# Output products of a hybrid encoder layer: which operand is halved where, one bank for the running sums, and a new order at both ends

## Chip, cores and metric

The kernel runs on one core of a Trainium2 chip. The metric is the device time of one execution in microseconds (us). Five engines work side by side, each through its own program in order: TensorE (PE in the profile; its weight loads, PEld, overlap the matmuls), VectorE (DVE), ScalarE (ACT), GpSimd (POOL) and SyncE (SP), which here issues the DMA transfers. They meet only in semaphores.

## What is computed

One encoder layer over x of 4096 rows by 1024:

```python
h = rmsnorm(x, pre_norm_g)
proj = h @ w_in                      # splits into q, k, v, g_a, u_p, g_p
a = banded_attention(q, k, v, rel_bias, sink) * silu(g_a)
p = multiscale_pool(u_p, pool_w, pool_scale) * silu(g_p)
mixed = concat([a, p]) @ w_out       # 1024 x 1024
x = x + rmsnorm(mixed, post_norm_g)
```

The attention is banded: each block of 128 queries sees its own block of keys and the two beside it, with a bias by distance and a sink term in the denominator. The pooling takes centred means over 2, 4, 8 and 16 rows, less the row itself.

## The kernel before

Every float32 operand of a matmul is split into a high and a low float16 part, and each product is high by high, high by low and low by high, summed in PSUM.

**First stage** (lines 135 to 796). It goes over x in eight macro-tiles of 512 rows. A tile of 128 rows is loaded (`x_load`), its mean square taken (`x_square`, `x_scale`), scaled and split (`x_high` on ScalarE, `x_low` on VectorE) and transposed by DMA (`x_turn`, line 193). Weight tiles are loaded (`w_load`), scaled by their column norm (`w_square`, `w_norm` on TensorE, `w_scale`, `w_scaled`) and split (`w_high`, `w_low`). Then 12 groups of 24 matmuls of 512 columns (`mm`, line 589) give the two gates and the pooling input; for the first macro-tile and first weight tile the matmuls run per 128 rows (`mm_first`, line 576), so that they can start on the first transposed tile. Gates and pooled blocks go to memory (`ga_scr`, `yp_scr`), and the output weights are brought into seven combinations for the second stage (`wo_scale`, `wo_sum1`, `wo_sum2`, `wo_keep`; into `w_scr`).

**Second stage** (from line 799). It goes over 32 blocks of 128 rows from the last to the first, in 16 pairs `u`. For each pair: projections of k, v and q (`do_kv`, `do_q`, line 831 and 965), two visits per block (`scores`, line 867, and a softmax in steps: `logits` on VectorE, line 888; `exps`, 899; `denominators`, 906; `probs` on ScalarE, 921; `rests` on VectorE, 929; `turn`, a DMA transpose issued by SP, 938), then `values` (1009) and `gate` (1017).

The output product of a pair is a 2 by 2 block product: its two row blocks by the two halves of K (attention and pooling), times the 2 by 2 blocks of `w_out`. It is done in seven products instead of eight, with sums of the operands: `sum1` to `sum4` build `s1` to `s4`, `pair` makes their high and low parts (`high` on ScalarE, `low` on GpSimd, line 1031), and `product` (line 1091) runs 12 matmuls of 512 columns. Before, the quarter named 11 is the attention of the odd block, 21 that of the even block, 12 and 22 are the pooled blocks. The blocks come in descending order, so the even block of a pair is ready last; products `11`, `22` and `12` do not need it, `s1` to `s4` do. The results are combined by `add` on VectorE (line 1123), squared, multiplied by the gain and added to x (`square`, `gain`, `mean`, `residual`, `store`).

**Order.** The order on all engines is written by hand: each step is put into `plan` by `due(t, step)`, and the steps are emitted in order of t. `pe(us, step)` puts a TensorE step at the running planned time `now[0]` and advances it; `visit` also keeps scores apart by `free`. The planned times set nothing but the order: on the chip each engine runs its program in order and waits for its operands. Three PSUM banks (`acc0` to `acc2`) are shared by projections and products.

Of the kernel before, what the change touches and what calls it, by code (L numbers as in the profile page):

```python
# [66 lines left out]
def hybrid_layer(ctx: ExitStack, tc, io, out):  # L67
# [67 lines left out]
    with ExitStack() as actx:  # L135
# [297 lines left out]
        def wo_load(kk):  # L433
            wo_t[kk] = pa.tile([P, D], F32, name=f"wo_b{kk}", tag="wraw", bufs=W_BUFS)
            nc.sync.dma_start(wo_t[kk], io["w_out"][kk])

        def wo_scale(kk):
            nc.scalar.activation(wo_t[kk], wo_t[kk], AF.Copy, scale=rowsc[:, kk : kk + 1])
# [203 lines left out]
        due(5.4, x_square, 0)  # L642
        due(6.6, w_square, 0)
        due(6.7, x_scale, 0)
        due(7.0, w_fold, 0, nc.gpsimd)
        due(7.6, x_high, 0)
        due(7.8, w_norm, 0, KT, gg)
        due(8.4, w_scale, 0)
        due(8.7, x_square, 1)
        due(8.8, x_low, 0)  # L650
        due(9.0, x_turn, 0)
        due(9.9, x_square, 2)
        due(10.0, x_scale, 1)
        due(10.4, w_scaled, 0)
        due(10.6, x_square, 3, nc.vector)
        due(10.7, w_high, 0)
        due(11.1, x_scale, 2)
        due(11.7, x_high, 1)
        due(11.8, w_low, 0)
        due(11.9, w_gate, 0)  # L660
        due(12.0, w_fold, 1, nc.gpsimd)
        due(12.8, x_low, 1)
        due(12.9, x_turn, 1)
        due(12.9, x_high, 2)
        due(13.0, x_scale, 3)
        due(14.2, x_low, 2)
        due(14.3, x_turn, 2)
        due(14.4, x_high, 3)
# [5 lines left out]
        due(14.35, lambda: nc.sync.dma_start(pw, io["pool_w"].rearrange("j p c -> p j c")))  # L674
        for j in range(2):
            due(15.9 + 0.1 * j, u_load, j)
        for i in range(BPM):
            due(14.0 + 1.3 * i + 1.5 * (i > 0), mm_first, i)
        due(15.5, w_norm, 1, KT)
        due(17.6, w_scale, 1)  # L680
        w_steps(1, 22.4)
        fold(2, 15.6)
        due(17.7, w_norm, 2, KT)
        due(18.8, w_scale, 2)
        w_steps(2, 25.0)
        fold(3, 18.8)
# [11 lines left out]
        def prepare(n):  # L698

            si = first[n + 2 :]  # L700
            if si:
                norm(si[0], 2 if A_GA <= si[0] < A_U else KT)
# [17 lines left out]
        now[0] = 21.0  # L720
        after(0, 0, 21.0)
# [258 lines left out]
    def proj_q(u, half):  # L980

        kv_t[u, half] = gemm.tile([P, 2, UT], F32, name=f"aq{u}_{half}", tag=f"acc{half}")
        for jj in range(2):
            project_t(kv_t[u, half][:, jj], B_Q + 2 * half + jj, x_half(u))
# [38 lines left out]
    def high(u, name, f):  # L1023

        tag = {"12": "s1", "22": "s3"}.get(name, name)
        y_t[u, name] = pb.tile([P, 4, 2, P], F16, name=f"y{name}_{u}", tag=f"y{tag}", bufs=1)
        nc.scalar.copy(y_t[u, name][:, :, 0], f(u))  # L1027

    def low(u, name, f):
        y = y_t[u, name]  # L1030
        nc.gpsimd.tensor_tensor(out=y[:, :, 1], in0=f(u), in1=y[:, :, 0], op=ALU.subtract)
# [5 lines left out]
    def a11(u):  # L1037
        return at[2 * u + 1]

    def a21(u):  # L1040
        return at[2 * u]

    def a12(u):
        return yf[u, 1]

    def a22(u):
        return yf[u, 0]

    def a_s1(u):
        return yf[u, 2]  # L1050
# [6 lines left out]

    def sum1(u):
        yf[u, 2] = pb.tile([P, 4, P], F32, name=f"s1_{u}", tag="s1", bufs=1)
        nc.vector.tensor_tensor(out=yf[u, 2], in0=a21(u), in1=a22(u), op=ALU.add)  # L1060

    def sum3(u):
        nc.vector.tensor_tensor(out=a21(u), in0=a21(u), in1=a11(u), op=ALU.subtract)

    def sum2(u):
        nc.vector.tensor_tensor(out=a11(u), in0=a_s1(u), in1=a11(u), op=ALU.subtract)

    def sum4(u):
        nc.gpsimd.tensor_tensor(out=a12(u), in0=a12(u), in1=a11(u), op=ALU.subtract)

    def sums(u, t):
        due(t, sum1, u)
        due(t + 0.05, sum3, u)
        due(t + 0.1, sum2, u)
        pair(t + 1.4, u, "s2", a11)
        pair(t + (10.0 if u > 1 else 2.0 + 2.0 * u), u, "s3", a21)
        pair(t + (10.6 if u > 1 else 2.6 + 2.0 * u), u, "s1", a_s1)
        due(t + 5.0, sum4, u)
        pair(t + (11.3 if u > 1 else 7.0), u, "s4", a12)
# [3 lines left out]
    def product(u, name, o, tag, acc=None):  # L1083

        y = y_t.pop((u, name))
        if acc is None:
            z_t[u, tag] = gemm.tile([P, 512], F32, name=f"m{name}_{u}", tag=f"acc{tag}")
        n = 0
        for k in range(HK):
            for yi, wi in ((0, 0), (0, 1), (1, 0)):  # L1090
                nc.tensor.matmul(  # L1091
                    z_t[u, tag], y[:, k, yi, :], wo[o][:, wi, k, :],
                    start=(n == 0 and acc is None), stop=(n == 3 * HK - 1),
                    skip_group_check=True,
                )
                n += 1

    def begin(u):
        mo_t[u] = [pb.tile([P, D], F32, name=f"mo{u}_{i}", tag=f"mo{i}", bufs=1) for i in range(2)]
        ss_t[u] = pb.tile([P, 4], F32, name=f"ss{u}", tag="ss")  # L1100
        nc.scalar.copy(mo_t[u][0][:, HI], z_t[u, 0])  # L1101
# [8 lines left out]
    def gain11(u):  # L1110
        nc.vector.tensor_tensor(
            out=mo_t[u][0][:, LO], in0=z_t[u, 0], in1=gpost[:, LO], op=ALU.mult
        )

    def gain(u, i, cs):
        mo = mo_t[u][i][:, cs]
        eng = nc.gpsimd if u else nc.vector
        eng.tensor_tensor(out=mo, in0=mo, in1=gpost[:, cs], op=ALU.mult)  # L1118

    def add(u, dst, src, bank):  # L1120
        (i, c), (k, e) = dst, src
        mo = mo_t[u]
        nc.vector.tensor_tensor(out=mo[i][:, c], in0=z_t[u, bank], in1=mo[k][:, e], op=ALU.add)  # L1123

    def load_xr(u, i):
        b = 2 * u + 1 - i
# [13 lines left out]
    def residual(u, i, cs):  # L1140
        xr = xr_t[2 * u + 1 - i][:, cs]
# [4 lines left out]
    def store(u, i, cs):  # L1146
        b = 2 * u + 1 - i
# [20 lines left out]
    free = [0.0, 0.0]  # L1168

    def visit(b, half):  # L1170
# [3 lines left out]
        free[:] = t + 2.9, t + 7.9  # L1174
# [10 lines left out]
    def attend(b):  # L1185
        t = pe(2.1, values, b)
        due(t, gate, b)
        if b % 2:
            pair(t + 0.8, b // 2, "11", a11)
        else:  # L1190
            sums(b // 2, t + 0.7)
# [3 lines left out]
    def mix_p1(u):  # L1195
        due(pe(M, product, u, "11", O11, 0) - 2.0, begin, u)

    def mix_p4(u):
        pe(M, product, u, "22", OT4, 2)

    def mix_p2(u):
        t = pe(M, product, u, "12", O21, 0, True)
        due(t, square, u, 0, 0, 0)
        due(t + 0.1, gain11, u)

    def mix_p6(u):
        due(pe(M, product, u, "s2", OT2, 1), add, u, (0, HI), (0, HI), 1)

    def mix_p7(u):
        t = pe(M, product, u, "s3", OT3, 0)  # L1210
        due(t - 2.0, add, u, (1, HI), (0, HI), 0)
        due(t - 1.9, add, u, (1, LO), (1, HI), 2)
        due(t + 1.4, square, u, 1, 0)
        due(t + 2.0, gain, u, 1, LO)

    def mix_p5(u):
        t = pe(M, product, u, "s1", OT1, 1)
        due(t, add, u, (1, HI), (1, HI), 1)
        due(t + 0.7, square, u, 1, 1)
        due(t + 1.4, gain, u, 1, HI)  # L1220
        finish(u, 1, t + (1.5 if u == 0 else 4.0))

    def mix_p3(u):
        t = pe(M, product, u, "s4", O22, 1, True)
        due(t, add, u, (0, HI), (0, HI), 1)
        due(t + 0.7, square, u, 0, 1)
        due(t + 1.4, gain, u, 0, HI)
        finish(u, 0, t + (1.5 if u == 0 else 4.0))

    def finish(u, i, t):  # L1230

        due(t, mean, u, i)
        for n, cs in enumerate((LO, HI) if u == 0 else (slice(0, D),)):
# [4 lines left out]

    u = NU - 1
    for o in (OT4, O11, O21, OT2):  # L1240
        due(0.0, load_wo, o)
    due(0.1, load_gain)
    due(0.1, pool_in, u, 0)
    due(0.1, pool_in, u, 1)
# [4 lines left out]
    now[0] += 1.0  # L1249
    for b in reversed(range(NB)):  # L1250
# [3 lines left out]
        if b % 2 == 0 and 0 < b < NB - 2:  # L1254
            due(t0 + 9.0, load_xr, u + 1, 1)
            due(t0 + 9.0, load_xr, u + 1, 0)
        if b > 0:
            visit(b, 0)
        if b == NB - 1:
            do_q(u, 1, 2.8)  # L1260
            due(now[0] + 0.1, load_x, u - 2)
            now[0] += 2.5
            visit(b, 1)
            do_kv(u - 1, 2, 2.5)
            now[0] += 3.0
        elif b == NB - 3:
            due(free[1], load_wo, OT3)
            mix_p4(u + 1)
            mix_p1(u + 1)
            attend(b + 1)  # L1270
            visit(b, 1)
            due(free[1], load_wo, OT1)
            due(free[1] + 8.0, load_wo, O22)
            do_kv(u - 1, 1)
            mix_p2(u + 1)
            mix_p6(u + 1)
        elif b == 1:
            mix_p3(u + 2)
            mix_p4(u + 1)
            visit(b, 1)  # L1280
            attend(b + 1)
            mix_p1(u + 1)
            mix_p2(u + 1)
            visit(b - 1, 0)
            mix_p6(u + 1)
        elif b % 2:
            mix_p3(u + 2)
            do_kv(u - 1)
            attend(b + 1)
            visit(b, 1)  # L1290
            mix_p1(u + 1)
            mix_p4(u + 1)
            mix_p2(u + 1)
            mix_p6(u + 1)
        elif b:
            do_q(u - 1, 0, 2.0 * (b == NB - 2))
# [119 lines left out]
```

## Time and profile before

| | us |
|---|---|
| median of 3 runs (lowest, highest) | 1260.27 (1259.67, 1261.21) |
| the profiled execution's own time | 1259.69 |
| its span, first to last instruction | 1257.9 |
| TensorE busy / VectorE / ScalarE / GpSimd | 1209.9 / 813.5 / 633.3 / 378.6 |
| first stage's last projection, second stage's first | about 540 |

The profile is of one execution. The granted TensorE clock was 0.995 of full speed on the mean. A line of the time order gives start and duration in us, the engine, the line of the kernel, the operation, output and inputs, how many instructions were merged, and in brackets the idle time of the engine before and what ended it. "SPq" is SP's queue of DMA issues: the duration there is that of issuing, not of the transfer.

### The profile page before, as it was taken

The page shows a single profiled execution, that of the slowest core. Times are in us where ns is not written, and L with a number is a line of the kernel's source. Part 1 is how long each engine was busy: PE and PEld are TensorE (multiplying, and loading weights), DVE is VectorE, ACT ScalarE, POOL GpSimd, SP SyncE. Part 2 cuts the span into 40 slices and gives each one's busy share as a digit, 9 for nine tenths or more (in the row PEclk, how much of TensorE's full clock was granted, in tenths as well). Part 3 has the DMA queues.
Part 4 walks back from the last instruction along what each step waited for, and adds up shares of the span by engine and source line. Part 5 has one row for each costly group of instructions (what it writes and reads, how often), then busy time and mean ns, then how long its engine had stood idle before and what let it go on. Part 6 is the DMA issues. An engine that isn't in the chain of part 4 may idle for free. (4 is left out here: it accounts for less than half of the span.)

```text
span 1257.9 us, 22182 instructions
## 1 busy us (share of the span) xinstructions
PE 1209.9 (96%) x8614; PEld 703.3 (56%) x8614; DVE 813.5 (65%) x1712; ACT 633.3 (50%) x1350; POOL 378.6 (30%) x378
## 2 busy tenths in 40 slices
PE   3999999999999999999999999999999999999975
PEld 3644444444444444476676766676666667675632
DVE  5564444445356564437778777877787787778774
ACT  4462424243435351146656666676567556756651
POOL 3132121211020201201244434433533453344442
PEclk9999999999999999999999999999999999999998
DMA  8364647486668683176957866776777678666753
GB/s 248 145 155 125 160 143 168 157 210 215 169 194 232 224 238 109 59 240 130 278 118 190 196 159 158 193 185 135 193 194 168 131 181 205 169 133 158 155 148 117
DMA packets 337753, 216.48 MB, mean 172 GB/s; under 512 B 266944, under 2 KB 308544, under 8 KB 334064
## 3 DMA queue, kind: packets, MB, share of 16 engines
q1 hardware_dynamic: 337648, 215.07, 64.4%
q8 instruction: 67, 1.10, 0.3%
q14 instruction: 38, 0.31, 0.1%
HBM read 93.38 MB, written 56.13 MB: 119 GB/s over the span
## 5 line engine op out<-in xcount | busy, mean ns | idle before, releaser
L589 PE MATMUL a<-xt,wa_h 128*128 128x512 f16 x1520 | 455.5, 379 | 0.0
L589 PE MATMUL a<-xt,wa_l 128*128 128x512 f16 x760 | 288.0, 379 | 0.0
L589 PEld LDWEIGHTS <-wa_h 128*128 128x128 f16 x1520 | 148.7, 98 | 178.4 <-issue 0.9
L899 ACT ACTIVATE p<-p,nm 128x385 f32<-128x385 f32 (+1 forms) x256 | 153.1, 600 | 64.2 <-POOL p L882 39.8
L1091 PE MATMUL ms<-wo,ys 128*128 128x512 f16 x768 | 173.9, 379 | 4.8 <-ACT pn L921 1.5
L929 DVE SCALAR_TENSOR_TENSOR pn<-p,rd,pn 128x384 f16<-128x384 f32 (+1 forms) x256 | 161.1, 675 | 24.4 <-ACT pn L921 24.4
L831 PE MATMUL aq<-xt,wb_h 128*128 128x256 f16 x1024 | 173.1, 273 | 0.0
L888 DVE CUSTOM_DVE_ANT_0 p<-s,bias,nsink 128x384 f32<-128x384 f32 (+1 forms) x256 | 156.2, 666 | 1.3 <-PE s L867 1.0
L921 ACT ACTIVATE pn<-p,rd 128x384 f16<-128x384 f32 (+1 forms) x256 | 136.6, 596 | 25.2 <-ACT p L899 24.1
L831 PE MATMUL aq<-xt,wb_l 128*128 128x256 f16 x512 | 139.5, 273 | 0.0
L831 PEld LDWEIGHTS <-wb_h 128*128 128x128 f16 x1280 | 125.2, 98 | 24.9 <-issue 9.3
L1091 PE MATMUL m<-wo,y 128*128 128x512 f16 x576 | 130.2, 384 | 3.1 <-ACT mo L1101 1.8
L1091 PEld LDWEIGHTS <-ys 128*128 128x128 f16 x768 | 73.7, 98 | 93.9 <-issue 7.4
L589 PEld LDWEIGHTS <-wa_l 128*128 128x128 f16 x760 | 74.4, 98 | 87.8
L554 POOL TENSOR_TENSOR yt<-yt,s 128x512 f32<-128x512 f32 x32 | 47.7, 1490 | 229.7 <-DVE yt L547 103.8
L493 ACT ACTIVATE s<-a,cg 128x512 f32<-128x512 f32 x63 | 42.5, 682 | 134.6 <-PE a L589 128.6
L498 DVE SCALAR_TENSOR_TENSOR s<-a,s 128x512 f32<-128x512 f32 x63 | 42.9, 688 | 101.7 <-ACT s L493 95.4
L1118 POOL TENSOR_TENSOR mo<-mo,gpost 128x512 f32<-128x512 f32 x45 | 74.2, 1648 | 101.1 <-ACT jkb L1106 100.0
L1091 PEld LDWEIGHTS <-y 128*128 128x128 f16 x576 | 55.3, 99 | 74.0 <-issue 9.3
L186 DVE SCALAR_TENSOR_TENSOR xp<-xn,rs,xp 128x1024 f16<-128x1024 f32 x32 | 44.3, 1385 | 56.8 <-ACT xp L183 56.8
L867 PE MATMUL s<-k_all,q 64*128 64x384 f16 (+2 forms) x912 | 73.2, 296 | 5.3 <-DVE nm L888 2.5
L1009 PE MATMUL o<-pt,vv 128*64 128x256 f16 x1128 | 68.8, 276 | 7.1 <-DMA pt<-pn 7.1
(135 smaller groups left out, 1541.3 us busy)
## 6 DMA issues: line engine op xcount, KB each, us to landing
xn<-in_x SPq DMA_DIRECT2D x32, 512.0 KB, 4.4
xr<-in_x SPq DMA_DIRECT2D x32, 512.0 KB, 4.4
out<-xr SPq DMA_DIRECT2D x30, 512.0 KB, 3.6
x_scr<-xt SPq DMA_DIRECT2D x7, 2048.0 KB, 7.9
xt<-x_scr SPq DMA_DIRECT2D x14, 1024.0 KB, 7.8
ga_scr<-s SPq DMA_DIRECT2D x32, 256.0 KB, 2.6
yp_scr<-yt SPq DMA_DIRECT2D x32, 256.0 KB, 2.4
yf<-yp_scr SPq DMA_DIRECT2D x32, 256.0 KB, 2.9
```

The costliest lines, as they stand in the source:

```text
L186: nc.vector.scalar_tensor_tensor(out=x_p[b][:, 1], in0=x_n.pop(b), scalar=rs_t.pop(b), in1=x_p[b][:, 0], op0=ALU.mult, op1=ALU.subtract,)
L554: nc.gpsimd.tensor_tensor(out=t, in0=t, in1=g_t.pop((m, A_GP + j)), op=ALU.mult)
L589: nc.tensor.matmul(a3, w[:, si, k, :], x[:, :, kk, :], start=(n == 0), stop=(n == 3 * KT - 1))
L831: nc.tensor.matmul(a3, w[:, j, k, :], x[:, :, kk, :], start=(n == 0), stop=(n == 3 * KT - 1))
L867: nc.tensor.matmul(s_ps[:, gg, c0:c1], q_t[u, half][a, qi, jj, tl : tl + P], k_all[a, ki, kc : kc + c1 - c0], start=(n == 0 and c0 == 0), ...
L888: nc.vector.tensor_tensor_reduce(out=p_t[b, half][:, hh, :nk], in0=s_t[b, half][jj][:, gg, :nk], in1=bias[:, h, lo : lo + nk], scale=negc[ ...
L899: nc.scalar.activation(p[:, hh, : nk + 1], p[:, hh, : nk + 1], AF.Exp, bias=nm_t[b, half][:, hh : hh + 1], scale=-1.0, accum_out=den_t[b, ...
L921: nc.scalar.activation(prob_view(b, half)[:, 0, i], p_t[b, half][:, i, :nk], AF.Copy, scale=rd_t[b, half][:, i : i + 1],)
L929: nc.vector.scalar_tensor_tensor(out=pn4[:, 1, i], in0=p_t[b, half][:, i, :nk], scalar=rd_t[b, half][:, i : i + 1], in1=pn4[:, 0, i], op0= ...
L1009: nc.tensor.matmul(o_ps[a, 2 * half : 2 * half + 2], v[:, vi, kt, a], pt[b, half][:, pi, g, :, i, :], start=(n == 0), stop=(n == last),)
L1091: nc.tensor.matmul(z_t[u, tag], y[:, k, yi, :], wo[o][:, wi, k, :], start=(n == 0 and acc is None), stop=(n == 3 * HK - 1), skip_group_che ...
L1118: eng.tensor_tensor(out=mo, in0=mo, in1=gpost[:, cs], op=ALU.mult)
```

## The change

The quarters change places: 11 and 21 are now the pooled blocks, 12 and 22 the attention of the even and the odd block. So `11` and `s3` come from pooling alone, `22`, `s1` and `s2` need the odd block, and only `12` and `s4` need the even block. The halves of `w_out` are loaded the other way round to match (`wo_load`, `wo_scale`). `sum3` moves to GpSimd and `sum4` to VectorE.

Sums over products are made in PSUM: `11`, `s2`, `s1` and `s4` add up in one bank, `s3` and `22` in a second, `12` has the third; between them ScalarE copies the partial sum out (`take`, three per pair instead of one copy in `begin`), and there are three `add`s instead of five. A product that continues in a bank must wait for the copy of what stood there. `proj_q` moves from banks 0 and 1 to 1 and 2.

In each pair the products stand at other places among the projections and visits. At the begin of the second stage the next pair's `proj_k` stands before the first visit, the weights come one by one, 6 us apart; for the first and last blocks visits are planned 6.0 apart instead of 7.9. For the last pair five products stand before or around the last values, `12` and `s4` after. In the last pair two lows run on VectorE.

At the start of the first stage the third weight tile and the pooling weights are loaded behind the second weight tile, ahead of the transposes, the fourth weight tile after them; `w_fold` 1 goes from GpSimd to VectorE and behind its norm; `w_norm` 1 follows the first tile's matmuls, `w_norm` 2 the last tile's, and `w_norm` 3 moves behind the next group of matmuls.

```diff
-            nc.sync.dma_start(wo_t[kk], io["w_out"][kk])
+            nc.sync.dma_start(wo_t[kk], io["w_out"][(kk + HK) % KT])
...
-        due(0.1, w_load, 0, io["w_a"][0])
-        due(0.5, w_load, 1, io["w_a"][1])
+        for t, si in ((0.1, 0), (0.5, 1), (0.6, 2), (20.0, 3)):
+            due(t, w_load, si, io["w_a"][si])
...
-        due(12.0, w_fold, 1, nc.gpsimd)
-        due(12.8, x_low, 1)
...
-        due(15.5, x_low, 3)
-        due(15.5, w_square, 1)
-        due(15.6, x_turn, 3)
-        due(9.1, w_load, 2, io["w_a"][2])
-        due(12.95, w_load, 3, io["w_a"][3])
-        due(14.35, lambda: nc.sync.dma_start(pw, io["pool_w"].rearrange("j p c -> p j c")))
...
+        due(13.3, w_square, 1)
...
+        due(16.0, w_norm, 1, KT, gg)
+        due(16.8, w_scale, 1)
+        due(16.9, x_low, 3)
+        due(17.0, x_turn, 3)
+        due(18.1, w_scaled, 1)
+        due(18.2, w_fold, 1)
...
+        due(21.6, w_norm, 2, KT)
...
+        due(0.7, lambda: nc.sync.dma_start(pw, io["pool_w"].rearrange("j p c -> p j c")))
...
+        for i, t in enumerate((14.9, 18.0, 19.5, 21.0)):
+            due(t, mm_first, i)
...
     def a11(u):
+        return yf[u, 0]
+
+    def a21(u):
+        return yf[u, 1]
+
+    def a12(u):
+        return at[2 * u]
+
+    def a22(u):
         return at[2 * u + 1]
...
+    def sum3(u):
+        yf[u, 2] = pb.tile([P, 4, P], F32, name=f"s3_{u}", tag="s3", bufs=1)
+        nc.gpsimd.tensor_tensor(out=yf[u, 2], in0=a21(u), in1=a11(u), op=ALU.subtract)
+
     def sum1(u):
+        nc.vector.tensor_tensor(out=a21(u), in0=a21(u), in1=a22(u), op=ALU.add)
 
     def sum2(u):
+        nc.vector.tensor_tensor(out=a11(u), in0=a21(u), in1=a11(u), op=ALU.subtract)
 
     def sum4(u):
+        nc.vector.tensor_tensor(out=a11(u), in0=a12(u), in1=a11(u), op=ALU.subtract)
...
+    def take(u, i, c, bank):
+        nc.scalar.copy(mo_t[u][i][:, c], z_t[u, bank])
...
+    def pooled(u, t, wait=0.0):
+
+        due(t, pool_in, u, 0)
+        due(t + 0.1, pool_in, u, 1)
+        due(t + wait + 4.5, sum3, u)
+        pair(t + wait + 5.0, u, "11", a11)
+        pair(t + wait + 7.0, u, "s3", a_s3)
+
+    def attend(b, wait=0.0):
         t = pe(2.1, values, b)
+        u = b // 2
         due(t, gate, b)
         if b % 2:
+            due(t + 0.7, sum1, u)
+            due(t + 0.75, sum2, u)
+            gap = 2.0 if u > 1 else 1.0
+            pair(t + wait + 1.0 + 0.5 * gap, u, "s2", a11)
+            pair(t + wait + 1.0 + 1.5 * gap, u, "s1", a21)
+            pair(t + (wait + 1.0 + 2.5 * gap if u else 0.8), u, "22", a22)
         else:
+            pair(t + wait + 0.7, u, "12", a12)
+            due(t + wait + 0.8, sum4, u)
+            pair(t + (wait + 1.5 if u else 3.0), u, "s4", a11)
...
+        if b == NB - 1:
+            pe(2.6, proj_k, u - 1, 0)
+            due(now[0] + 1.0, keep_k, u - 1)
+            visit(b, 0)
+            do_q(u, 1)
+            visit(b, 1)
+            due(pe(2.8, proj_v, u - 1) + 1.0, keep_v, u - 1)
...
+        elif b % 2 and b > 1:
...
             visit(b, 0)
+            mix_p6(u + 1)
+            do_kv(u - 1)
+            mix_p5(u + 1)
             attend(b + 1)
             visit(b, 1)
             mix_p4(u + 1)
             mix_p2(u + 1)
+            mix_p3(u + 1)
+        elif b > 1:
+            pooled(u, t0 + 0.5)
+            visit(b, 0)
+            do_q(u - 1, 0)
+            attend(b + 1, 6.0 if u > 1 else 1.0)
             visit(b, 1)
+            do_q(u - 1, 1)
             due(now[0] + 2.1, load_x, u - 3)
+            if u > 1:
+                mix_p1(u)
+                mix_p7(u)
+        elif b == 1:
...
+            visit(0, 0)
+            pooled(0, now[0], 2.0)
+            mix_p2(1)
+            mix_p3(1)
+        else:
+            visit(0, 1)
             attend(1)
+            mix_p1(0)
+            mix_p7(0)
             mix_p4(0)
...
+            mix_p6(0)
             attend(0)
+            mix_p5(0)
             mix_p2(0)
             mix_p3(0)
```

More of the change, by code (lines that the diff above doesn't have):

```diff
@@ L1209, in mix_p7 @@
[L1209 to L1221, printed above, removed]
-    def mix_p3(u):
[L1224 to L1228, printed above, removed]
+        t = pe(M, product, u, "12", O21, 2)
```

285 lines of the change are left out of this document (117 added, 168 removed).

## The prediction

> **What bounds the kernel now.** I read the page's busy times first, then the busy times in stretches (per engine: busy us and instruction count; then granted clock, DMA share, GB/s), then TensorE's waits.
>
> ```profile
> PE 1209.9 (96%) x8614; PEld 703.3 (56%) x8614; DVE 813.5 (65%) x1712; ACT 633.3 (50%) x1350; POOL 378.6 (30%) x378
> 0.00:35.00 35.00, 15.52 (x145) 14.93 (x146) 18.03 (x37) 17.27 (x21) 12.76 (x14) 0.95 0.82 233
> 35.00:550.00 515.00, 515.00 (x2516) 242.30 (x2514) 256.82 (x473) 183.96 (x244) 93.80 (x97) 1.00 0.58 172
> 550.00:605.00 55.00, 48.87 (x480) 35.18 (x479) 36.88 (x99) 34.67 (x90) 8.63 (x11) 1.00 0.67 171
> 605.00:1190.00 585.00, 584.99 (x5210) 389.28 (x5206) 458.43 (x1024) 371.38 (x930) 237.70 (x233) 1.00 0.71 173
> 1190.00:1250.00 60.00, 45.53 (x276) 21.59 (x272) 39.31 (x76) 25.33 (x66) 24.71 (x24) 0.94 0.47 132
> 1250.00:1257.90 7.90, 0.00 (x0) 0.00 (x0) 4.07 (x7) 0.72 (x2) 0.99 (x1) 0.79 0.36 134
> ```
>
> TensorE is the bound: busy 1209.9 of 1257.9 us. Its 48.0 us of idle time lie in four places: 19.5 (35.00 less 15.52) at the start, 6.1 where the second stage begins, 14.5 before 1250, 7.9 after it. From 35 to 550 and from 605 to 1190 it never waits. The change leaves TensorE's work as it is: seven products of 12 matmuls, the same projections, scores and values per pair of blocks. So it can only win in those four places, and can only lose by opening a wait in the full stretches.
>
> **Start.** What released TensorE there, then the instructions in order of time (start, duration, engine, line, in brackets the idle time before and its releaser), and last the transposes' median time to landing.
>
> ```profile
> PE n L264 <- ACT sq L249: 10.3, 2, 7.5
> PE gp L576 <- DMA xt<-xp: 9.1, 2, 6.4
> ...
> 14.93 1.87 PE L576 MATMUL gp<-xt,wa_h 128*128 128x128 f16 x16 [6.39 <-DMA xt<-xp]
> 18.99 3.56 SPq L193 DMA_TRANSPOSE xt<-xp  x1
> 19.42 1.28 DVE L186 SCALAR_TENSOR_TENSOR xp<-xn,rs,xp 128x1024 f16<-128x1024 f32 x1 [1.62 <-ACT xp L183]
> 20.39 1.01 PE L264 MATMUL n<-sq,ones 128*128 128x128 bf16 x8 [2.74 <-ACT sq L249]
> 22.60 0.58 SPq L674 DMA_DIRECT2D pw<-in_pool_w  x1
> 23.28 3.02 SPq L193 DMA_TRANSPOSE xt<-xp  x1
> 29.45 1.86 PE L576 MATMUL gp<-xt,wa_h 128*128 128x128 f16 x16 [2.73 <-DMA xt<-xp]
> 34.85 0.38 PE L589 MATMUL a<-xt,wa_h 128*128 128x512 f16 x1
> xt<-xp SPq DMA_TRANSPOSE x4, 5.7
> ```
>
> The fourth tile's transpose is what ends last: its input was ready at 20.70 (19.42 + 1.28), but SP was still issuing the third transpose until 22.55 and then the load of `pw`, so it went out at 23.28 and TensorE waited until 29.45. The change puts `w_load` 2 and `pw` ahead of the transposes (0.75 MB; estimate from the 512 KB tiles already queued there: under 1 us for the first transpose) and 3 behind them. `x_low` 3 gains nothing: `w_scale` 1 now stands ahead of it on VectorE and waits for `w_norm` 1, which follows the first tile's matmuls (14.93, then 24 matmuls of which 16 took 1.87, then 1.0 for the norm, about 0.7 to read and reduce it, and 1.3): 20.4 to 20.8 again. Its transpose goes out when the third has been issued, between 20.7 and 22.2 instead of 23.28, and lands 5 to 6 us later, at 25.7 to 28.2. I take 26.6: 2.8 us sooner. `w_norm` 3 leaves this stretch for the next, where it costs 0.5 of those 2.8. **Gain 2.4, bounds -1 and 4**: below nothing if the earlier loads delay the first transpose; 4 if TensorE's waits for the first three close too.
>
> **Beginning of the second stage.** TensorE's waits from 540 to 610 us (total, times, longest):
>
> ```profile
> PE ms L1091 <- ACT pn L921: 1.5, 1, 1.5
> PE s L867 <- ACT q L820: 1.4, 2, 0.7
> PE o L1009 <- DMA pt<-pn: 1.1, 1, 1.1
> PE s L867 <- DVE q L821: 0.9, 2, 0.4
> ```
>
> The first scores waited for the two halves of q, 1.15 us each time. The change puts `proj_k` (2.6 us planned) behind the first `proj_q`, which covers one of them. The second stays. The values of block 31 come 11.8 us after its last scores (planned: `proj_v` 2.8, `proj_q` 5.3, scores 1.1, `mix_p1` 2.6), and the one product before them has its input from the pooling alone. I keep 1.2 to 3 of 6.1. **Gain 4.5, bounds 3 and 5.** The loads of `wo` are spread by 6 us each and have no reader within 20 us, so I cost them at nothing; late, they would add one landing wait.
>
> **The full stretch.** This is where the change can lose. One odd block of before, its second half, and the median landing of `pt`:
>
> ```profile
> 721.62 1.50 DVE L1142 SCALAR_TENSOR_TENSOR xr<-mo,rs,xr 128x1024 f32<-128x1024 f32 x1
> 721.64 1.16 PE L867 MATMUL s<-k_all,q 64*128 64x256 f16 x24
> 725.44 0.69 DVE L1066 TENSOR_TENSOR at<-s,at 128x512 f32<-128x512 f32 x1
> 726.05 0.67 DVE L888 CUSTOM_DVE_ANT_0 p<-s,bias,nsink 128x384 f32<-128x384 f32 x1
> 731.48 2.21 DVE L929 SCALAR_TENSOR_TENSOR pn<-p,rd,pn 128x384 f16<-128x384 f32 x4 [0.73 <-ACT pn L921]
> 733.75 3.69 SPq L938 DMA_TRANSPOSE pt<-pn  x1
> 739.67 2.16 PE L1009 MATMUL o<-pt,vv 128*64 128x256 f16 x36
> ...
> pt<-pn SPq DMA_TRANSPOSE x55, 6.2
> ```
>
> From the end of the scores (722.80) to the transpose took 10.95 us, and to landing 10.95 + 6.2 = 17.15. TensorE had 16.9 us of other work before these values, and 1.1 more before the second half of them: no wait. After the change only `mix_p4`, `p2`, `p3` (7.8 by the code's planned figures), one visit's scores (1.1) and `proj_q` (5.3) lie between: 14.2, with the 1.1 makes 15.3. So the chain must shrink by 1.85 us. It does: the softmax started 3.25 us late (726.05) behind the residual, the gate and three sums; now the gate and one sum (`sum4`, 0.69) stand there, so it starts about 0.75 after the scores, 2.5 sooner. Inserted are two adds (0.69 each) and two squares between exps and probs; each delays it by 0.3 to 0.7. I get a transpose 8.6 to 9.1 after the scores and landing at 14.8 to 15.3, against 15.3. **I take a loss of 0.1 us in each of 14 pairs, 1.5 in all, bounds 0 and 10.** VectorE loses two adds, ScalarE gains two copies per pair; neither is near its limit over 605 to 1190 (78% and 63%). The `take` copies that now free a bank before the next product sums into it have `mix_p7` with scores, or `do_kv`, as cover, at least 3.7 us for a 0.6 us copy. In the last pair `mix_p4` follows `mix_p7` in the same bank without cover: below.
>
> Two rows bear on how safe that is (GpSimd gain against VectorE rests):
>
> ```profile
> 758.83 2.37 POOL L1118 TENSOR_TENSOR mo<-mo,gpost 128x512 f32<-128x512 f32 x1
> 759.98 2.16 DVE L929 SCALAR_TENSOR_TENSOR pn<-p,rd,pn 128x384 f16<-128x384 f32 x2
> ```
>
> Two rests took 2.16 instead of 1.1 (half of the 2.21 above) while GpSimd ran: 1.0 us for one such meeting. In the new order two gains and two lows fall into the chain. One meeting more than I counted costs 0.5 to 0.9 us per pair. The Trainium skill (SBUF — State Buffer, "Who interferes with whom") says that a VectorE instruction with two SBUF inputs contends with a GpSimd instruction that reads SBUF, and that the second one to start blocks fully; by that rule the rests would wait for whole gains, and the sum would be that of the second rival.
>
> **End.**
>
> ```profile
> 1196.42 2.75 PE L1091 MATMUL m<-wo,y 128*128 128x512 f16 x12 [1.76 <-ACT mo L1101]
> 1204.62 1.26 POOL L1069 TENSOR_TENSOR yf<-yf,at 128x512 f32<-128x512 f32 x1
> 1227.51 1.90 SPq L938 DMA_TRANSPOSE pt<-pn  x1
> 1231.87 1.49 PE L1009 MATMUL o<-pt,vv 128*64 128x256 f16 x12 [6.00 <-DMA pt<-pn]
> 1233.29 4.86 PE L1091 MATMUL m<-wo,y 128*128 128x512 f16 x12
> 1246.98 2.75 PE L1091 MATMUL ms<-wo,ys 128*128 128x512 f16 x12 [1.06 <-DVE mo L1123]
> 1253.29 1.41 DVE L1142 SCALAR_TENSOR_TENSOR xr<-mo,rs,xr 128x512 f32<-128x512 f32 x2 [0.45 <-POOL rs L1138]
> yf<-yp_scr SPq DMA_DIRECT2D x28, 256.0 KB, 2.9
> ```
>
> Before, the end costs 14.2 us of waits up to TensorE's end at 1249.73, 8.2 from there to 1257.9, and 2.1 because the 12 matmuls behind the 6 us wait took 4.86 instead of 2.75: 24.5. After it, five of the last pair's seven products do not need block 0: four of them (10.4 us), with the values of block 1 (2.1), cover the last softmax. I ordered the last two blocks by their due times. TensorE still waits: 0.5 for `pt` of block 1; 2.2 at `mix_p1(0)`, because `pool_in` stands on SP behind a 3.7 us transpose issue, lands 2.9 later, and GpSimd then runs `sum3` (1.26) before the low; 1.1 at `mix_p7(0)`, whose low stands on GpSimd behind the power of the other row block; 1.1 at `mix_p4(0)` for the copy (the 1.76 wait above is the same pattern). Sum 4.9, bounds 2.5 and 10. None is near 6 us, so the slow matmuls go. The tail loses the add between the last matmul and the square (0.7), and the last residuals wait no longer behind it (0.45): 7.0. **Gain 24.5 - 4.9 - 7.0 = 12.6, bounds 8 and 15.**
>
> **Sum.** 2.4 + 4.5 + 12.6 - 1.5 = 18.0 from the profiled execution's 1259.69 us (span 1257.9): 1241.7. The median of the runs is 0.6 above that execution, so 1242.3; I say 1242.
>
> **Rivals.**
> 1. *A new wait per pair, slower.* If the chain of the odd block's second half keeps its measured 17.15 us, TensorE waits 1.85 us at the values in each of 14 pairs: 25.9 lost against 19.5 gained elsewhere, 1267. It decides from 1.4 us per pair. For: the cover shrinks by 2.7 us; GpSimd's interference. Against: the three sums ahead of it are gone, in plain program order. Chance 0.11.
> 2. *Part of it.* One meeting with GpSimd more, 0.5 to 0.9 us per pair: 7 to 12 lost, 1248 to 1254. Chance 0.17.
> 3. *The end moves less than it says.* ScalarE's and GpSimd's in-order queues hold the last softmax behind pooling data, so that block 0 comes last anyway: 5 to 8 us of the 12.6 stay, 1247 to 1250. For: the lines of the last pair stand on ScalarE between the last exps. Against: 10 us of cover. Chance 0.11.
>
> My forecast (1235 to 1247) has 0.58; 0.03 is left for gains and losses that cancel. Differences within 0.2% (2.5 us) count as the same, about what a measurement of this kernel can tell from no change. Faster 0.86, same 0.03, slower 0.11. The range takes in rivals 2 and 3: 1235 to 1254; only for the forecast itself it is 1235 to 1247.
>
> **What would show it.** Right: the fourth tile's matmuls start at 26 to 28; under 3 us idle from 550 to 605; none for `pt` from 605 to 1190; no 6 us wait at the last values, the last matmuls at 0.22 us spacing, 7 us from TensorE's end to the span's. Wrong: a `pt` wait that recurs every 43 us (rivals 1 and 2), or a wait over 3 us behind 1190 (rival 3). The number is wrong, the mechanism not, if `pool_in` comes earlier or later than I placed it.

## The result and the profile after

The changed kernel is slower: 1271.59 us at the median of five runs (1270.54 to 1274.05) against 1260.27 (1259.11 to 1261.26) of the kernel before, ratio 1.0089 (95% interval 1.0076 to 1.0102). Forecast were 1242 and a range of 1235 to 1254, so the direction was wrong too. The profile below is of one execution (1272.31 us, span 1270.5).

The page's busy times, then the stretches (length, then busy us and count of PE, PEld, DVE, ACT, POOL; then granted clock, DMA share, GB/s) of the kernel after:

```profile
PE 1209.5 (95%) x8614; PEld 698.3 (55%) x8614; DVE 814.4 (64%) x1679; ACT 646.8 (51%) x1382; POOL 367.1 (29%) x378
```

```profile
0.00:35.00 35.00, 16.23 (x156) 13.79 (x157) 19.25 (x37) 18.38 (x21) 9.56 (x12) 1.00 0.89 248
...
550.00:605.00 55.00, 52.30 (x480) 35.46 (x478) 38.27 (x98) 34.59 (x92) 9.67 (x11) 1.00 0.78 223
605.00:1190.00 585.00, 564.35 (x5010) 372.18 (x5005) 439.91 (x955) 365.92 (x915) 217.79 (x224) 1.00 0.63 163
1190.00:1262.00 72.00, 60.01 (x434) 32.48 (x433) 57.28 (x113) 41.83 (x107) 29.98 (x29) 0.98 0.59 151
1262.00:1270.50 8.50, 1.62 (x8) 0.54 (x6) 3.51 (x5) 1.27 (x4) 2.24 (x2) 0.85 0.32 123
```

TensorE does the same work (1209.5 us busy). The fourth row is the result: from 605 to 1190 it is idle for 20.6 us (585.00 less 564.35), where it never waited before. What released it there (total, times, longest):

```profile
PE m L1088 <- ACT mo L1100: 18.4, 13, 2.2
PE m L1088 <- POOL ys L1036: 2.2, 13, 0.2
```

Thirteen waits of some 1.4 us, one per pair, all for ScalarE's `take` (line 1100), and none for `pt`. The short POOL wait is inside the same product, for its low part. Measured from one `proj_v` of a pair to the next in the time order, a pair takes 44.6 us instead of 42.9.

The other three places, first matmuls of the fourth tile and of the first 512-wide group, then the waits from 540 to 610, then those behind 1190:

```profile
27.21 1.05 PE L577 MATMUL gp<-xt,wa_h 128*128 128x128 f16 x16 [3.63 <-DMA xt<-xp]
...
30.84 0.38 PE L590 MATMUL a<-xt,wa_h 128*128 128x512 f16 x1
```

```profile
PE o L1013 <- DMA pt<-pn: 1.5, 1, 1.5
PE s L871 <- ACT q L824: 0.7, 1, 0.7
PE s L871 <- DVE q L825: 0.4, 1, 0.4
```

```profile
PE ms L1088 <- POOL ys L1036: 2.6, 1, 2.6
PE s L871 <- DVE nm L892: 2.5, 2, 1.9
PE m L1088 <- POOL y L1036: 2.3, 1, 2.3
PE m L1088 <- ACT mo L1100: 1.6, 1, 1.6
PE o L1013 <- DMA pt<-pn: 1.5, 1, 1.5
...
```

The 512-wide group starts 4.0 us sooner (34.85 before), the beginning of the second stage idles 2.7 us instead of 6.1, and the end has no 6 us wait any more, but five of 1.5 to 2.6.

**Where the wait per pair comes from.** One pair of the kernel after, TensorE and then ScalarE in order of time (start, duration; in brackets the idle time before):

```profile
758.43 2.75 PE L1088 MATMUL ms<-wo,ys 128*128 128x512 f16 x12
761.11 1.15 PE L871 MATMUL s<-k_all,q 64*128 64x384 f16 x12
763.60 0.59 PE L1088 MATMUL m<-wo,ys 128*128 128x512 f16 x2 [1.34 <-ACT mo L1100]
764.36 2.33 PE L1088 MATMUL m<-wo,ys 128*128 128x512 f16 x10 [0.17 <-POOL ys L1036]
```

```profile
748.43 0.62 ACT L1031 CAST y<-yf 128x512 f16<-128x512 f32 x1 [1.26 <-DMA yf<-yp_scr]
...
757.43 0.62 ACT L903 ACTIVATE p<-p,nm 128x385 f32<-128x385 f32 x1 [5.36 <-DVE nm L892]
...
760.43 2.13 ACT L925 ACTIVATE pn<-p,rd 128x384 f16<-128x384 f32 x4
762.47 0.60 ACT L1031 CAST ys<-yf 128x512 f16<-128x512 f32 x1
762.98 0.57 ACT L1100 COPY mo<-m 128x512 f32<-128x512 f32 x1
```

`mix_p1` was done at 758.6. Behind it TensorE had `mix_p7` and scores until 762.26: 3.7 us of cover, as forecast. But the copy began only at 762.98, 4.4 us after its input was there. ScalarE was not busy in that time for itself: it stood idle for 5.36 us ahead of 757.43, and everything behind, the copy too, came late. What it waited for is on VectorE:

```profile
749.60 1.58 DVE L933 SCALAR_TENSOR_TENSOR pn<-p,rd,pn 128x384 f16<-128x384 f32 x1 [0.80 <-ACT pn L925]
...
751.70 2.87 DVE L933 SCALAR_TENSOR_TENSOR pn<-p,rd,pn 128x384 f16<-128x384 f32 x3
754.49 0.68 DVE L1021 TENSOR_TENSOR at<-o,gb 128x512 f32<-128x512 f32 x1
755.26 0.69 DVE L1068 TENSOR_TENSOR yf<-yf,at 128x512 f32<-128x512 f32 x1
756.05 0.69 DVE L1071 TENSOR_TENSOR yf<-yf,yf 128x512 f32<-128x512 f32 x1
756.65 0.67 DVE L892 CUSTOM_DVE_ANT_0 p<-s,bias,nsink 128x384 f32<-128x384 f32 x1
```

The scores of the second half of the even block ended at 750.66; their logits (756.65) came 6.0 us later, behind four rests, the gate, `sum1` and `sum2`. The same place in the kernel before, TensorE and then VectorE:

```profile
741.76 1.15 PE L867 MATMUL s<-k_all,q 64*128 64x384 f16 x12
```

```profile
744.50 0.69 DVE L1017 TENSOR_TENSOR at<-o,gb 128x512 f32<-128x512 f32 x1
745.11 0.67 DVE L888 CUSTOM_DVE_ANT_0 p<-s,bias,nsink 128x384 f32<-128x384 f32 x1
```

There the scores ended at 742.91 and the logits followed by 2.2 us, directly behind the gate. In the kernel after the rests themselves were late because ScalarE, ahead of the probs, had waited 1.26 us for a pooled load, which SP issued only at 745.59, behind a transpose whose issue began at 741.83 and took 3.66 us. **Theory:** VectorE's and ScalarE's queues at this place, not the copy or its bank, make the wait. **Rivals:** the shared bank; the late pooled loads alone.

### The profile page after: what moved, and what is told of

It reads as the page before. It is cut to its first block, busy times and chain, and to the rows that moved or that the text cites. A ratio compares the mean times of both kernels' runs of the same rounds, so it can differ in the third digit from the quotient of the medians.

```text
span 1270.5 us, 22160 instructions
## 1 busy us (share of the span) xinstructions
PE 1209.5 (95%) x8614; PEld 698.3 (55%) x8614; DVE 814.4 (64%) x1679; ACT 646.8 (51%) x1382; POOL 367.1 (29%) x378
## 5 line engine op out<-in xcount | busy, mean ns | idle before, releaser
L933 DVE SCALAR_TENSOR_TENSOR pn<-p,rd,pn 128x384 f16<-128x384 f32 (+1 forms) x256 | 190.5, 788 | 35.5 <-ACT pn L925 33.8
L1088 PE MATMUL m<-wo,ys 128*128 128x512 f16 x576 | 136.1, 382 | 22.5 <-ACT mo L1100 20.1
L1116 POOL TENSOR_TENSOR mo<-mo,gpost 128x512 f32<-128x512 f32 x48 | 62.6, 1304 | 171.4 <-ACT jkb L1105 171.4
L499 DVE SCALAR_TENSOR_TENSOR s<-a,s 128x512 f32<-128x512 f32 x63 | 42.9, 687 | 104.1 <-ACT s L494 97.6
L1036 POOL TENSOR_TENSOR ys<-yf,ys 128x512 f16<-128x512 f32 x47 | 54.5, 1172 | 137.0 <-ACT ys L1031 132.4
L1088 PE MATMUL m<-wo,y 128*128 128x512 f16 x384 | 88.5, 379 | 2.8 <-POOL y L1036 2.3
```

Of the source, the lines that this page charges most:

```text
L933: nc.vector.scalar_tensor_tensor(out=pn4[:, 1, i], in0=p_t[b, half][:, i, :nk], scalar=rd_t[b, half][:, i : i + 1], in1=pn4[:, 0, i], op0= ...
L1036: eng.tensor_tensor(out=y[:, :, 1], in0=f(u), in1=y[:, :, 0], op=ALU.subtract)
L1088: nc.tensor.matmul(z_t[u, i], y[:, k, yi, :], wo[o][:, wi, k, :], start=(n == 0 and not acc), stop=(n == 3 * HK - 1), skip_group_check=True,)
L1116: nc.gpsimd.tensor_tensor(out=mo, in0=mo, in1=gpost[:, cs], op=ALU.mult)
```

## Experiments

All ratios are against the kernel before, run on the same chip.

**1. The start alone.** The kernel before with the new order of the first stage's start, and nothing else:

```diff
-        due(0.1, w_load, 0, io["w_a"][0])
-        due(0.5, w_load, 1, io["w_a"][1])
+        for t, si in ((0.1, 0), (0.5, 1), (0.6, 2), (20.0, 3)):
+            due(t, w_load, si, io["w_a"][si])
...
+        due(16.0, w_norm, 1, KT, gg)
```

> The kernel before with the new start of the first stage alone. In the trace of the changed kernel the first full group of matmuls began at 30.84 us instead of 34.85, with 0.5 us of norm matmuls moved behind it. Theory: these 3.5 us are kept, because TensorE never waits between 35 and 550 us: 1256.8 us (1256 to 1257.5). Rival: they are given back by later waits for the weights that now come later: 1259 to 1261.

Measured 1257.75, ratio 0.9983 (0.9974 to 0.9993): 1.9 us, 0.25 above the upper end. Most of the start's term holds; the 3.5 us of the expectation come from one execution with a full clock at the start, and the profile of this run has 0.90 there.

**2. A bank of its own for `mix_p6`.** In pairs 2 to 15 `s2` no longer waits for the bank of `11`, so that product 11 stays out of three of the four quarters there; the k and v projections and product 12 take the bank that this frees:

```diff
-        t = pe(M, product, u, "s2", OT2, 0, True)
+        t = pe(M, product, u, "s2", OT2, 0, u < 2, 2 if u > 1 else None)
...
-        t = pe(M, product, u, "12", O21, 2)
+        t = pe(M, product, u, "12", O21, 2, False, 0 if u > 1 else None)
...
-            do_kv(u - 1)
+            do_kv(u - 1, 0)
```

> The changed kernel, but in the 14 pairs before the last two the product s2 starts in a bank of its own (the third; the k and v projections and the product 12 take the first), so that it need not wait for ScalarE's copy of the product 11. It leaves the product 11 out of the sums of three of the four output quarters in these pairs. Theory (a late queue): the high and low parts of s2 come from the same late ScalarE queue, the low ends 0.75 us after the copy, so the wait stays at about 1.3 to 1.7 us a pair: 1267 to 1272 us. Rival (the shared bank): the wait is for the bank alone, 20 us go: 1249 to 1253 us.

Measured 1275.12, ratio 1.0123 (1.0108 to 1.0138), 3.1 us above the range of the theory and further from the rival. The wait stayed as long and changed its name, to the two parts of `s2` (605 to 1190):

```profile
PE ms L1089 <- ACT ys L1031: 11.9, 13, 1.3
PE ms L1089 <- POOL ys L1036: 8.2, 13, 0.6
```

So the shared bank is not the cause: what stands beside the copy on ScalarE is equally late. The 3.1 us lie outside these waits and are not placed.

**3. `sum3` and the parts of 11 and s3 4 us later.** (In pairs 1 to 14 the parts of 11 are then made behind `sum2`, which has overwritten their buffer: product 11 works on the operand of `s2` there. The instructions are the same.)

```diff
-            pooled(u, t0 + 0.5)
+            pooled(u, t0 + 0.5, 4.0)
```

> The changed kernel, but in the pairs before the last the difference s3 and the high and low parts of 11 and s3 are due 4 us later, behind the first half's softmax; the loads stay. Theory (a late queue): the first half's probs no longer wait on ScalarE for pooled data, its rests on VectorE no longer meet GpSimd, the second half's logits start 3 to 4 us sooner, the copy and the parts of s2 come in time, and the wait at product s2 goes: 1247 to 1254 us. Rival (the shared bank): the copy still ends too late, 1268 to 1272 us.

Measured 1247.35, ratio 0.9908 (0.9892 to 0.9925). The wait per pair is gone, although `sum1` and `sum2` still stand ahead of the logits: without the pooled parts in ScalarE's queue ahead of the probs the logits follow their scores by 3.6 us, and that is early enough.

**4. Only the loads 4 us sooner.**

```diff
-            pooled(u, t0 + 0.5)
+            pooled(u, t0 - 3.5, 4.0)
```

> The changed kernel, but in the pairs before the last the two loads of pooled blocks are due 4 us sooner, ahead of the transpose behind which they stood on SP; the sums and parts stay where they were due. Theory, if the late data are the larger part of the delay: the wait at product s2 goes, 1248 to 1254 us. If GpSimd's interference with the rests on VectorE is the larger part: the rests stay slow (about 5 us instead of 2.2 for four), 0.5 to 1.2 us of wait stay a pair, 1256 to 1266 us. Rival (the shared bank): 1268 to 1272 us.

Measured 1267.48, ratio 1.0065 (1.0050 to 1.0080), between the two ranges of 1256 to 1266 and 1268 to 1272. The loads are the smaller part.

**5. Only `sum1` and `sum2` behind the logits.** (Here and in 6, 7 and 9 pair 15 is moved too, where the parts of `s2` come ahead of the sums: that one product of that pair works on an operand not yet summed. Where the expectations say otherwise, they are wrong.)

```diff
-            due(t + 0.7, sum1, u)
-            due(t + 0.75, sum2, u)
+            late = 3.6 if u > 1 else 0.7
+            due(t + late, sum1, u)
+            due(t + late + 0.05, sum2, u)
```

> The kernel after, with one move in the 14 pairs with u > 1: sum1 and sum2 (0.69 us each, 2.07 with the gate and the steps between) stand on VectorE behind the four logits of the even block's second half instead of ahead of them. Theory (the wait of mix_p6 comes from ScalarE's queue, which starts the exps late because VectorE reaches the logits late): the logits come 1.4 us sooner, the copy that frees the bank and the parts of s2 as well, and the wait of 1.3 to 1.7 us per pair shrinks to under 0.4: 1249 to 1255 us, time at the copy in 605 to 1190 under 5 us. Rival (ScalarE is held by the pooled parts, whose loads land late, and GpSimd by their lows; the sums are only beside it): the wait stays over 1 us per pair, 1264 to 1272.

Measured 1256.40, ratio 0.9970 (0.9959 to 0.9982), 1.4 us above the upper end. The waits from 605 to 1190:

```profile
PE m L1088 <- ACT mo L1100: 3.5, 10, 0.8
PE m L1088 <- POOL ys L1036: 2.2, 13, 0.2
```

**6. The sums behind the logits and `sum3` and the parts 3 us later.**

```diff
+        late = 3.0 if u > 1 else 0.0
-        due(t + wait + 4.5, sum3, u)
-        pair(t + wait + 5.0, u, "11", a11)
-        pair(t + wait + 7.0, u, "s3", a_s3)
+        due(t + wait + late + 4.5, sum3, u)
+        pair(t + wait + late + 5.0, u, "11", a11)
+        pair(t + wait + late + 7.0, u, "s3", a_s3)
...
```

> As the one before, and sum3 and the parts of 11 and s3 are due 3 us later in the 14 pairs with u > 1, so that they do not fall beside the rests of the even block's first half. Computes what the reference does. Theory (VectorE late by the sums and by the meeting with GpSimd): no wait of mix_p6 at all in 605 to 1190, idle there under 3 us, 1245 to 1249 us. Rival (it is the total load of ScalarE in the odd block, or the copy itself): the wait moves to another place of the same pair, over 0.8 us each, 1257 or more.

Measured 1247.31, ratio 0.9901 (0.9885 to 0.9918), as the theory had it. The same place of a pair, ScalarE and then TensorE:

```profile
743.50 0.60 ACT L1031 CAST y<-yf 128x512 f16<-128x512 f32 x1
747.74 0.62 ACT L903 ACTIVATE p<-p,nm 128x385 f32<-128x385 f32 x1 [3.63 <-DVE nm L892]
...
754.51 0.57 ACT L1100 COPY mo<-m 128x512 f32<-128x512 f32 x1
```

```profile
754.42 1.15 PE L871 MATMUL s<-k_all,q 64*128 64x384 f16 x12
755.51 2.76 PE L1088 MATMUL m<-wo,ys 128*128 128x512 f16 x12
```

The copy ends at 755.08, just ahead of the scores' end at 755.57. The logits now follow their scores by 3.0 us (743.97 to 746.97) instead of 6.0. Over the runs this delay and the time of a pair go together (medians of pairs 13 to 2): 6.0 us and 44.6 in the kernel after, 5.7 and 44.3 in experiment 4, 4.5 and 43.5 in 5, 4.1 and 43.15 in 7, 3.6 and 42.9 in 3, 3.0 and 42.9 here.

**7. The sums behind the logits and the loads sooner** (edits of 4 and 5).

> As the first of these, and the pooled loads are issued 4 us sooner, with sum3 and the parts where they were. If the late loads hold ScalarE (the cast of 11 waits until they land), this takes what the move of the sums leaves, 1247 to 1250. If the meeting of sum3 and the lows with VectorE's rests is what is left, it stays within 2 us of the kernel with the sums moved alone.

Measured 1251.82, ratio 0.9935 (0.9920 to 0.9950): 4.6 us below experiment 5, between what the two theories expected. The loads do hold ScalarE, but don't take all that is left. Pair by pair the shares add up: 44.6 us in the kernel after, 44.26 with the loads sooner, 43.5 with the sums moved, 43.15 with both, 42.87 with the sums and parts moved.

**8. As 6, with `sum1` and `sum2` of pair 15 left where the kernel after has them**, so that every product has the reference's operands. (Its `sum3` and parts still come 3 us later; where the expectation has all of pair 15 as in the kernel after, it is wrong.)

> The kernel after, with sum1 and sum2 behind the logits and sum3 and the parts of 11 and s3 3 us later in pairs 2 to 14 only; pairs 0, 1 and 15 as in the kernel after. Computes what the reference does. If pair 15 had no part in it, the time of the earlier kernel with both late in pairs 2 to 15: 1246.5 to 1248.

Measured 1248.59, ratio 0.9905 (0.9888 to 0.9921). It beats both kernels; about 1% below the kernel before.

**9. The end, three moves in the queues.** As 6, pair 1 treated likewise, the pooled loads of pair 0 ahead of block 1's second transpose on SP, its sums and parts ahead of a gain and a power on GpSimd, and `mix_p1(1)`'s copy ahead of the exps:

```diff
...
-            pooled(0, now[0], 2.0)
+            for i in range(2):
+                due(now[0] - 1.4 + 0.1 * i, pool_in, 0, i)
+            pair(now[0] + 3.4, 0, "11", a11)
+            due(now[0] + 4.6, sum3, 0)
+            pair(now[0] + 6.0, 0, "s3", a_s3)
```

> As the second of these, with the same treatment of pair 1 and three moves in the end: the pooled loads of pair 0 stand on SP ahead of the transpose of block 1's second half, sum3 and the parts of 11 and s3 of pair 0 stand on GpSimd ahead of a gain and a power, and the copy of mix_p1(1) stands on ScalarE ahead of the exps of block 1. Computes what the reference does. Theory (the waits of the end are queue order and late loads, as the forecast's end had it in smaller sizes): the waits of scores(1,0) 2.5, mix_p6(1) 1.6 and mix_p1(0) 2.7 us and half of the 3.3 at mix_p7(0) and mix_p4(0) go, and with them the slow clock: 6 to 10 us below the second of these, 1237 to 1242. Rival (the last softmax and its transpose come last anyway, so that the time shows at values(1), values(0) or the tail instead): under 3 us below the second of these.

Measured 1249.87, ratio 0.9920 (0.9905 to 0.9935): not below 6 at all, the rival's side. The three waits shrank to 0.5 us or less and two others came (over the whole execution; 1.4 of the 5.8 lie where the second stage begins):

```profile
PE ms L1088 <- ACT mo L1100: 6.2, 1, 6.2
PE o L1013 <- DMA pt<-pn: 5.8, 3, 3.1
```

**10. The copy of `mix_p7(0)` ahead of the last probs and that of `mix_p1(0)` behind; two lows of pair 1 on VectorE.** From here on `sum1` and `sum2` of pair 15 stand where the kernel after has them.

```diff
-        due(t, take, u, 0, LO, 0)
+        due(t + (2.8 if u == 0 else 0.0), take, u, 0, LO, 0)
...
+        t = pe(M, product, u, "s3", OT3, 1)
+        due(t - (2.55 if u == 0 else 0.0), take, u, 1, HI, 1)
...
```

> The kernel with both ends treated, with two edits more in the end: the copy of mix_p7(0) stands on ScalarE ahead of the probs of block 0's second half, and that of mix_p1(0) behind them (there the two stood the other way round, and mix_p4(0) waited 6.2 us for the second of them); and VectorE instead of GpSimd makes the lows of 12 and s4 of pair 1. Computes what the reference does. Theory (the copy of mix_p1(0) waits for the last residual of pair 1, which reads the only buffer of that row block, and holds mix_p7(0)'s copy behind it; and GpSimd's lows beside the rests of block 1 make its transpose late): the 6.2 us go, the 3.1 us at values(1) fall under 2, and the clock stays full there: 1238 to 1243. Rival (the last softmax comes last anyway): the wait goes to values(0) or mix_p6(0), 1246 or more.

Measured 1248.48, ratio 0.9911 (0.9894 to 0.9927), the rival's side again. The 6.2 us became 1.8, half of the difference went to the values (4.4 to 6.6 us; 1.6 of the 8.2 lie where the second stage begins), and the stretch with most of pair 15's products took 0.8 us more than in 9 (43.64 against 42.84), its sums moved back:

```profile
PE o L1013 <- DMA pt<-pn: 8.2, 4, 2.7
...
PE ms L1088 <- ACT mo L1100: 1.8, 1, 1.8
```

**11. The same with the loads where the kernel after has them.**

> As the one before, with the pooled loads of pair 0, its sum3 and its parts of 11 and s3 where the kernel after has them, behind the transpose of block 1's second half. Computes what the reference does. By the theory that the loads' place costs mix_p1(0) its 2.7 us: 2 to 4 us more than the one before. By the rival that two loads ahead of the transpose cost values(1) what mix_p1(0) gains: within 1 us of it.

Measured 1247.99, ratio 0.9908 (0.9894 to 0.9923): within 0.5 us of 10. In the end the values wait 3.6 us instead of 6.6, and 3.5 us of waits for GpSimd's parts of 11 and s3 stand against it: what the loads' place gains at `mix_p1(0)` it costs at the values.

**12. As 11, three lows of pair 0 on VectorE instead of GpSimd.**

> The kernel with the end's edits and late loads, with the lows of 22, s2 and s1 of pair 0 on VectorE (0.69 us each) instead of GpSimd (1.15 to 2.14 there, beside the rests of the last softmax and the last residual of pair 1, which took 1.37 and 2.17 instead of 0.47 and 1.29). Computes what the reference does. Theory (the end is bound by VectorE's and GpSimd's work ahead of the last transpose, of which their meetings are a part): the last transpose is issued 1 to 2 us sooner and the time falls by 1 to 3 us. Rival (the transposes' issue and landing set the end, which no engine's work shortens): within 0.7 us of it.

Measured 1247.57, ratio 0.9899 (0.9884 to 0.9914): not told apart from 11.

**13. As 11, without the three GpSimd gains of pair 1.**

> The kernel with the end's edits and late loads, without the three GpSimd gains of pair 1 (1.3 to 1.8 us each; its rows are left without the post-norm gain on three of four quarters). Theory (as above: the rests of blocks 1 and 0 beside these gains take 1.4 to 1.6 us instead of 0.5, and the residual of row block 0 waits for the last of them): the rests are 2 to 3 us shorter in sum, the transposes of blocks 1 and 0 come 1 to 2 us sooner, 1244.5 to 1246.5. Rival (transposes' issue and landing): within 0.7 us of 1248.

Measured 1244.54, ratio 0.9876 (0.9860 to 0.9893), against 0.9908 (0.9894 to 0.9923): the one edit of the end that made it faster clear of noise, if narrowly. The last two transposes' issues on SP, with the gains (experiment 11) and without:

```profile
1214.78 2.00 SPq L942 DMA_TRANSPOSE pt<-pn  x1
...
1225.66 1.86 SPq L942 DMA_TRANSPOSE pt<-pn  x1
```

```profile
1212.11 2.02 SPq L942 DMA_TRANSPOSE pt<-pn  x1
...
1222.99 1.85 SPq L942 DMA_TRANSPOSE pt<-pn  x1
```

**14. As 11, these gains on VectorE.**

```diff
+        eng = nc.vector if u == 1 else nc.gpsimd
-        nc.gpsimd.tensor_tensor(out=mo, in0=mo, in1=gpost[:, cs], op=ALU.mult)
+        eng.tensor_tensor(out=mo, in0=mo, in1=gpost[:, cs], op=ALU.mult)
```

> The kernel with the end's edits and late loads (1247.99), with the three gains of pair 1 on VectorE (about 0.69 us each, 2.1 in sum) instead of GpSimd. Computes what the reference does. If the meetings of the gains with the rests set the end: 3.5 us gained as without the gains, less up to 2.1 for the work, 1245.5 to 1247. If the amount of work ahead of the last transposes sets it: no gain or a loss, 1248 to 1250.

Measured 1248.37, ratio 0.9898 (0.9884 to 0.9913): no gain that can be told from 11, and the last transpose went out at 1225.9, no sooner. Taking the gains away helps, moving them to VectorE does not: that points to the work of the two engines ahead of the last transposes as what sets the end. How much of it is their meetings and how much its amount stays open.

## Why the prediction was wrong

- **Start, 2.4 forecast.** Right: 1.9 by experiment 1. The fourth tile's matmuls began at 27.21, forecast 26 to 28; the first tile's came 1.2 us later (16.15 against 14.93), where the forecast took under 1. In the profiled execution of the kernel after the gain was 3.5 (4.0 less 0.5 for the moved norm), with the clock at 1.00 in that stretch instead of 0.95 before and 0.90 in experiment 1: part of the size is the luck of an execution.
- **Beginning of the second stage, 4.5 forecast, bounds 3 and 5.** Right in mechanism: 6.1 became 2.7, so 3.4. One wait for q (1.1) and one for `pt` (1.5) stayed.
- **Full stretch, 1.5 loss forecast, bounds 0 and 10. Here it failed.** Lost were 20.6 us of waits, 1.7 in 3.4 us at half clock (shown below), and 2.2 because the product that waited ran thirteen times in two pieces (0.59 and 2.33 us instead of 2.75 in one): 24.5. The step that failed is the sentence that the `take` copies "have `mix_p7` with scores, or `do_kv`, as cover, at least 3.7 us for a 0.6 us copy". The cover was there, 3.7 us to the decimal; the price set against it was the copy's duration, not its place in ScalarE's queue. That queue came 4.4 us late, because VectorE reached the even block's logits 6.0 us after the scores. What stood there anew: `sum1` and `sum2` (in the old order the sums stood ahead of the odd block's logits), the cast of 11 on ScalarE ahead of the probs, which waits for a pooled load that SP issues late, and GpSimd's `sum3` and lows beside the rests. The forecast followed this only for the odd block's chain, where the sums were gone; it didn't ask for the even block's, to which they went. The odd block's chain did come as forecast (scores' end 733.19, transpose 741.83: 8.6 us). Its working doesn't add up to that, though: four inserted steps of 0.3 to 0.7 us each on top of 10.95 less 2.5 make 9.7 to 11.3, not 8.6 to 9.1, so the agreement is in part luck. The bounds of 0 and 10 were drawn round the `pt` chain alone and so didn't contain the case.
- **Rival 1** had about the size (1267) but the wrong place: there was no wait for `pt` from 605 to 1190. **Rival 2** (a meeting with GpSimd more) is a part of it: the first rest took 1.58 us beside `sum3` instead of some 0.6.
- **End, 12.6 forecast, bounds 8 and 15. Wrong size:** waits, slow clock and tail were 24.5 by its count, and 25.1 with the twelve `values` matmuls at half clock that it left out (1.49 us at 1231.87 instead of the 0.84 of the twelve at 1225.02). They became 12.0 (72.00 less 60.01) + 1.7 (3.4 us at half clock) + 6.9 (8.50 less 1.62) = 20.6, so 4.5. The tail (7.0 forecast) and the missing 6 us wait were right. Wrong were the four small waits, counted one by one as 4.9 as if nothing else would come late: this is rival 3. Experiments 9 and 10 shrank most of them, and the sum came back elsewhere: the last transpose goes out at 1225.0 to 1225.7 in all of these (experiments 6 and 9 to 11), and the span ends 20 to 22 us behind it.
- **Sum.** Start 3.5, second stage 3.4, end 4.5 gained, 24.5 lost: 13.1 us longer, against 12.6 between the two spans; 0.5 is not placed. With the term that failed taken out again (experiment 8) the time is 1248.6, rival 3's figure: the end, 8 us short of its term, is most of what then keeps it from 1242.

## What to carry to other kernels

A copy, cast or low that is put on a path is priced by when its in-order engine gets to it, not by how long it takes: look for the last instruction on that engine that waits, and follow that one to what it waits for. When a change moves operations from one half of a period to the other, redo the chain of both halves; here the half that received them decided. And an end in which several small waits lie side by side can be one chain, as here: name the engine whose work fills the time between its last two steps before crediting any wait's removal.

## What the runs showed of the hardware

**The clock fell behind short waits.** TensorE in the kernel after, and two windows of it (the column behind the five engines is the granted clock):

```profile
628.19 0.59 PE L1088 MATMUL m<-wo,ys 128*128 128x512 f16 x2 [2.23 <-ACT mo L1100]
628.95 3.81 PE L1088 MATMUL m<-wo,ys 128*128 128x512 f16 x10 [0.17 <-POOL ys L1036]
```

```profile
629.60:633.10 3.50, 3.50 (x11) 1.40 (x10) 0.67 (x4) 1.87 (x8) 1.65 (x3) 0.51 1.04 196
1244.00:1247.50 3.50, 3.47 (x9) 1.27 (x10) 3.50 (x3) 1.78 (x4) 3.50 (x3) 0.51 0.37 150
```

A wait of 2.23 us was followed by some 3.4 us at half clock (a mean of 0.51 over 3.50 us), and so was one of 2.61 us at 1244; ten matmuls took 3.81 instead of 2.33 us. The forecast took "none is near 6 us" as enough to keep the clock. The Trainium skill (TensorE: Matmul & The Clock Gate, Part 1 on the HAM clock gate) puts the fall behind at least one idle window of about 3.4 us; here 2.23 us sufficed, while a wait of 2.30 us at 1238 (the third row of the end's waits) and the twelve waits of under 1.5 us in the long stretch did not lower it. Nor do the other runs show a length that decides: in experiment 2 waits of 1.26 and 0.64 us (ended 810.87 and 812.11) were followed by a clock of 0.50 from 812.3 to 815.6 and ten matmuls of 4.02 us, in experiment 7 waits of 1.68 and 0.54 us (ended 1185.03 and 1186.23) by 0.50 from 1186.5 to 1189.8, while in the kernel before 0.71 and 1.82 us (ended 1208.71 and 1211.04) left it at 1.00 from 1211 to 1230. What decides stays open.

**VectorE beside GpSimd.** GpSimd's `sum3` in that pair of the kernel after:

```profile
749.50 1.26 POOL L1065 TENSOR_TENSOR s<-yf,yf 128x512 f32<-128x512 f32 x1 [2.30 <-DMA yf<-yp_scr]
```

The rest that began 0.10 us behind it took 1.58 us and ended at 751.18, 0.42 us after `sum3` did (750.76). The engines here meet not in semaphores alone. The Trainium skill (SBUF — State Buffer, "Who interferes with whom") calls the port pair that the two share an exclusive lock, with a VectorE instruction of two SBUF inputs contending with a GpSimd instruction that reads SBUF; this row agrees: the rest, the second to start, ended only behind the first.
